# Score-value products of a paired head moved to the front of the next head, pairs of groups with fewer joins in other banks, and inverse roots' steps on GpSimd

## Chip, cores and metric

The kernel runs on one core of one Trainium2 chip. The metric is the device time of one execution in microseconds. Five engines of the core matter: TensorE (PE, with its weight loads as PEld), VectorE (DVE), ScalarE (ACT), GpSimd (POOL) and SyncE (SP, which here only issues loads).

## What is computed

A decoder trunk of two layers on 256 tokens of width 2048: first gated linear attention (GLA, 4 heads), then retention (8 heads), each after an RMS norm and with a SiLU gate; a residual add ends each layer and an RMS norm ends the trunk. Cut to what the change touches, a retention layer is

```
proj = rms_norm(h) @ w_in                    # q, k, v, gate
q, k = rotary(q), rotary(k)
o = (causal decay mask * (q @ k.T)) @ v      # per head, chunkwise in the reference
o = (o - mean(o)) * rsqrt(var(o) + EPS)      # per head, the "inverse root"
o = o * gn_g + gn_b
h = h + (o * silu(gate)) @ w_out
```

A GLA head has an inverse root too, rsqrt(mean(o*o) + EPS).

## The kernel before

**Weights and splits.** All weight matrices lie in DRAM as groups of 512 output columns. A group has 16 tiles of 128x512 (4 MB). SP loads it in chunks of 4 tiles (`raw`, four buffers). A chunk is cut into two units of 2 tiles. Each unit is split into a high and a low part in a rounded 32-bit type: ACT copies `hi` (L216), DVE subtracts to give `lo` (L217), both into pools of three buffers. The product of x and w is then three matmuls, xh·hi, xh·lo and xl·hi, in this order within a bank (L277 to L279 in pairs, L256 to L258 in plain groups). Splits are issued two units ahead of their use (`LOOK`).

**Pairs.** Two groups p and q that multiply the same input are done with seven block products in place of eight (`pair_x`), with token halves as rows and the first half of the contraction as the part that is recombined. `PAIR` is the order by hand: blocks `S1` to `S7` are one product of 12 matmuls each (two units), blocks `V0` to `V3` and `G0` to `G3` are plain products of one unit for both token halves, 12 matmuls each. Four results are wanted: 11 and 21 of group p, 12 and 22 of group q. Some block products are needed in several results, so they are taken out of PSUM and added elsewhere. These additions are called joins here. They are driven by events ("p1" after S1, "q" after S5, "p2" after S6, "p3" after S7, and "11", "21", "12", "22" when a bank is complete). PSUM has eight banks: pool `acc` with four, `lev` with two, `mis` with two. Where S5 or S6 need it, the weights of q are added onto the raw chunk of p in SBUF by an accumulating DMA that POOL issues (L225), after the split that last read the chunk. `token_combos` makes the recombined inputs.

**Where pairs are used.** In both output projections (`out_half`: "ga" and "gb" after GLA, "ra" and "rb" after retention, seven pairs in all, results added into the residual `R["t"]`) and in six retention heads (`paired`: h = 0, 1, 2, 4, 5, 6), where p is the value group and q the gate group. Heads 3 and 7 do the two groups in the plain way.

**A retention head.** `group_w` makes q and k of the head in eight units of 16 matmuls (units j = 0 to 7). `evac_w` takes them out of PSUM. `ret_scores` (rotary products L1040 to L1045, score matmuls, mask) runs as a generator on the `side` queue, a step at each `advance()`. Then the pair gives value and gate. The score-value products (`o_mms`, nine matmuls), the norm, the inverse root (`rsqrt`, L439 to L444, then L1114), the scaling (L1116) and `og_part` (gate product L1124, eight transposes L651, split L657 and L658 into `ogt`) of a paired head are held in `waiting` and run inside the `group_w` of the next head, at j = 3. GLA heads do their inverse root in `og_part` at L835.

**Order.** The order on each engine is fixed when the program is built: a scheduler walks the operations with priorities, so a later operation can be put ahead of an earlier one on the same engine. On the chip each engine takes its instructions strictly in that order. POOL's queue holds accumulating DMAs of weights, loads of small tables (L1047, L1093, L1094, L937), copies of the residual and 14 additions for each GLA head (L782).

## Time and profile before

| | before |
|---|---|
| median of 3 runs | 1401.64 us (1401.49 to 1404.17) |
| profiled execution, its own time | 1399.42 us |
| its span, first to last instruction | 1397.6 us |
| PE busy | 1372.5 us (98%) |
| DVE busy | 1070.9 us (77%) |
| ACT busy | 797.1 us (57%) |
| POOL busy | 144.7 us (10%) |
| mean granted TensorE clock | 0.998 |

The profiled execution took 1.8 us more than its span. A matmul's end in the profile is modelled: a 512-column matmul shows about 0.39 us although the next one can start 0.23 us after it, so the idle time that the profile gives for PE is a little shorter than what a stop costs.

### The profile page before, as it was taken

The page shows a single profiled execution, that of the slowest core. Times are in us where ns is not written, and L with a number is a line of the kernel's source. Part 1 is how long each engine was busy: PE and PEld are TensorE (multiplying, and loading weights), DVE is VectorE, ACT ScalarE, POOL GpSimd, SP SyncE. Part 2 cuts the span into 40 slices and gives each one's busy share as a digit, 9 for nine tenths or more (in the row PEclk, how much of TensorE's full clock was granted, in tenths as well). Part 3 has the DMA queues.
Part 4 walks back from the last instruction along what each step waited for, and adds up shares of the span by engine and source line. Part 5 has one row for each costly group of instructions (what it writes and reads, how often), then busy time and mean ns, then how long its engine had stood idle before and what let it go on. Part 6 is the DMA issues. An engine that isn't in the chain of part 4 may idle for free.

```text
span 1397.6 us, 17891 instructions
## 1 busy us (share of the span) xinstructions
PE 1372.5 (98%) x6644; PEld 1147.9 (82%) x6644; DVE 1070.9 (77%) x1619; ACT 797.1 (57%) x1012; POOL 144.7 (10%) x209
## 2 busy tenths in 40 slices
PE   8999999999999999999999999999999999999997
PEld 7888888788888888887887878888787878788887
DVE  6595798787845784888878787898777888888783
ACT  6665655755555646665665656456556565645563
POOL 1000030110010020111011111001201010100200
PEclk9999999999999999999999999999999999999999
DMA  9554555898545555799796969569989797974981
GB/s 370 192 185 147 193 180 181 203 296 266 174 175 181 185 195 183 188 297 277 231 276 201 273 202 304 208 198 268 278 291 237 238 234 240 233 306 165 234 297 61
DMA packets 54631, 316.04 MB, mean 226 GB/s; under 512 B 6400, under 2 KB 6912, under 8 KB 25232
## 3 DMA queue, kind: packets, MB, share of 16 engines
q1 hardware_dynamic: 34944, 243.42, 48.4%
q0 software_dynamic: 18592, 70.13, 24.7%
q10 hardware_dynamic: 1008, 1.35, 0.3%
q8 instruction: 52, 0.85, 0.2%
q14 instruction: 35, 0.29, 0.1%
HBM read 308.58 MB, written 6.29 MB: 225 GB/s over the span
## 4 chain that ended last, share of the span: by engine, by line
PE 92%; DVE 3%; DMA 2%; ACT 2%; issue 1%; ACTq 0%; POOLq 0%; DVEq 0%
PE rqk_ps L420 8%; PE rp__ps L278 4%; PE rp__ps L279 4%; PE gv_ps L256 4%; PE rp__ps L277 4%; PE gv_ps L257 4%; PE gv_ps L258 4%; PE gg_ps L256 4%; PE gg_ps L258 4%; PE gg_ps L257 4%; PE rqk_ps L421 4%; PE gqk_ps L420 4%; PE gqk_ps L421 2%; DMA raw<-in_w_all 2%; DVE lo L217 2%; ACT hi L216 1%
## 5 line engine op out<-in xcount | busy, mean ns | idle before, releaser
L216 ACT ACTIVATE hi<-raw 128x1024 fp32r<-128x1024 f32 (+1 forms) x551 | 580.0, 1058 | 503.4 <-PE rp__ps L279 80.8
L217 DVE TENSOR_TENSOR lo<-raw,hi 128x1024 fp32r<-128x1024 f32 (+1 forms) x551 | 666.0, 1222 | 256.2 <-ACT hi L216 251.6
L420 PE MATMUL rqk_ps<-xhl,hi 128*128 128x512 f32 x480 | 161.5, 394 | 0.0
L225 POOL DMA_DIRECT2D raw<-in_w_all x104 | 88.4, 850 | 470.0 <-DVE lo L217 430.8
L421 PE MATMUL rqk_ps<-xhl,lo 128*128 128x256 f32 x480 | 120.9, 280 | 0.0
L420 PEld LDWEIGHTS rqk_ps<-xhl,hi 128*128 128x128 f32 x480 | 88.0, 188 | 16.8
L257 PE MATMUL gv_ps<-lo,xhl 128*128 128x512 f32 x256 | 100.4, 392 | 0.0
L257 PE MATMUL gg_ps<-lo,xhl 128*128 128x512 f32 x256 | 100.4, 392 | 0.0
L258 PE MATMUL gv_ps<-hi,xhl 128*128 128x512 f32 x256 | 100.3, 392 | 0.0
L258 PE MATMUL gg_ps<-hi,xhl 128*128 128x512 f32 x256 | 100.0, 391 | 0.0
L278 PE MATMUL rp__ps<-lo,xhl 128*128 128x512 f32 x240 | 94.1, 392 | 2.6 <-DVE lo L217 2.6
L279 PE MATMUL rp__ps<-hi,xhl 128*128 128x512 f32 x240 | 93.5, 389 | 0.0
L256 PE MATMUL gv_ps<-hi,xhl 128*128 128x512 f32 x256 | 93.0, 391 | 0.0
L421 PEld LDWEIGHTS rqk_ps<-xhl,lo 128*128 128x128 f32 x480 | 87.8, 188 | 5.0
L256 PE MATMUL gg_ps<-hi,xhl 128*128 128x512 f32 x256 | 91.7, 391 | 0.0
L277 PE MATMUL rp__ps<-hi,xhl 128*128 128x512 f32 x240 | 85.2, 390 | 2.8 <-ACT hi L216 2.8
L420 PE MATMUL gqk_ps<-xhl,hi 128*128 128x512 f32 x216 | 72.4, 396 | 0.0
L782 POOL TENSOR_TENSOR s<-s,m 128x64 f32<-128x64 f32 x56 | 32.3, 610 | 241.5 <-DVE m L773 230.8
L278 PEld LDWEIGHTS rp__ps<-lo,xhl 128*128 128x128 f32 x240 | 45.1, 188 | 13.6 <-DVE lo L217 4.6
L257 PEld LDWEIGHTS gv_ps<-lo,xhl 128*128 128x128 f32 x256 | 48.1, 188 | 9.7
L257 PEld LDWEIGHTS gg_ps<-lo,xhl 128*128 128x128 f32 x256 | 48.1, 188 | 9.6
L258 PEld LDWEIGHTS gg_ps<-hi,xhl 128*128 128x128 f32 x256 | 48.1, 188 | 9.6
(461 smaller groups left out, 2694.3 us busy)
## 6 DMA issues: line engine op xcount, KB each, us to landing
raw<-in_w_all SPq DMA_DIRECT2D x225, 1024.0 KB, 4.9
raw<-in_w_all POOLq DMA_DIRECT2D x104, 512.0 KB, 7.2
held<-resid POOLq DMA_DIRECT2D x4, 1024.0 KB, 10.5
resid<-held POOLq DMA_DIRECT2D x2, 2048.0 KB, 12.2
resid<-in_x_n SPq DMA_DIRECT2D x2, 1024.0 KB, 11.2
gg<-in_gn_g POOLq DMA_DIRECT2D x8, 256.0 KB, 3.8
gb<-in_gn_b POOLq DMA_DIRECT2D x8, 256.0 KB, 4.5
raw<-in_w_all SPq DMA_DIRECT2D x3, 512.0 KB, 6.1
```

Source lines behind the costliest of these rows:

```text
L216: a = nc.scalar.activation(hi[:, sl], src[:, sl], AF.Copy)
L217: b = nc.vector.tensor_tensor(lo[:, sl], src[:, sl], hi[:, sl].bitcast(F32), ALU.subtract)
L225: nc.gpsimd.dma_start(src, chunk_src(g, k)[:, rows], accum_op=ALU.add)
L256: mm(ps, xh, hi[:, q, :], start=kt == 0, stop=False)
L257: mm(ps, xh, lo[:, q, :], start=False, stop=False)
L258: mm(ps, xl, hi[:, q, :], start=False, stop=kt == NKT - 1)
L277: mm(ps, xh, hi[:, q, :], start=start, stop=False, skip_group_check=True)
L278: mm(ps, xh, lo[:, q, :], start=False, stop=False, skip_group_check=True)
L279: mm(ps, xl, hi[:, q, :], start=False, stop=stop, skip_group_check=True)
L420: mm(ps[c], wh, rhs[:, kt, :, :], start=kt == 0, stop=False)
L421: mm(ps[c][:, 0, :], wl, rhs[:, kt, 0, :], start=False, stop=False)
L782: nc.gpsimd.tensor_tensor(dst, dst, side_of(m[:, li, :]), ALU.add)
```

## The change

The score-value products and all that follows them for a paired head are called at j = 0 of the next head's `group_w` in place of j = 3. The order of a pair puts V0 ahead of S2, and V0 does its second token half first. The first block product is copied by ACT from its bank into the bank of result 11, where V and S2 then accumulate, and result 22 accumulates in the bank that holds the product of S5. So the separate join of "p1" and one of the two joins of "q" are gone in `out_half`. In paired heads two DVE additions (in "p3" and "11") are gone, and the split of v's first half reads PSUM. The three steps of the iteration in `rsqrt` for GLA and retention heads run on GpSimd, four instructions a step in place of three on DVE, and so does the product L1114.

```diff
@@ -117,7 +117,7 @@
         for j in range(raws_per_group):
             plan_units(plan_chunk(g, j))
 
-    PAIR = ("S1", "S2", "V0", "V1", "S5", "S3", "V2", "G0", "S6", "G1", "S7", "V3", "S4", "G2", "G3")
+    PAIR = ("S1", "V0", "S2", "V1", "S5", "S3", "V2", "G0", "S6", "G1", "S7", "V3", "S4", "G2", "G3")
 
     def plan_pair(gp, gq):
         at = {}
@@ -342,16 +342,18 @@
         def mixed(n):
             return lambda k: tuple(x[:, k] for x in combos[cname][n])
 
-        def both(ps, j, start, stop):
+        def both(ps, j, start, stop, second_first=False):
             hi, lo = next_weights()
-            for q in range(SUB):
-                for t in range(2):
-                    kt = 2 * CHUNK + j * SUB + q
-                    x = tuple(lhs[:, kt, i, t * P : (t + 1) * P] for i in range(2))
-                    product(ps[t], x, hi, lo, q, start[t] and q == 0, stop[t] and q == SUB - 1)
+            order = [(q, t) for q in range(SUB) for t in range(2)]
+            if second_first:
+                order = [(q, t) for t in (1, 0) for q in range(SUB)]
+            for q, t in order:
+                kt = 2 * CHUNK + j * SUB + q
+                x = tuple(lhs[:, kt, i, t * P : (t + 1) * P] for i in range(2))
+                product(ps[t], x, hi, lo, q, start[t] and q == 0, stop[t] and q == SUB - 1)
             advance()
 
-        c21 = b = c12 = c22 = None
+        c21 = b = c12 = None
         for block in PAIR:
             kind, n = block[0], int(block[1])
             if kind == "V":
@@ -359,21 +361,20 @@
                     c21 = acc_p.tile([P, GW], F32, tag="acc", name=f"{name}_ps21")
                 if n == 2 and late is not None:
                     late()
-                both((c11, c21), n, (False, n == 0), (n == 3, False))
+                both((c11, c21), n, (False, n == 0), (n == 3, False), n == 0)
                 if n == 3:
                     on("11", c11)
             elif kind == "G":
-                if c22 is None:
-                    c22 = lev_p.tile([P, GW], F32, tag="lev", name=f"{name}_ps22")
-                both((c12, c22), n, (False, n == 0), (n == 3, n == 3))
+                both((c12, b), n, (False, False), (n == 3, n == 3))
                 if n == 3:
                     on("12", c12)
-                    on("22", c22)
+                    on("22", b)
             elif n == 1:
                 seven(a, plain(0, 0), True, True)
-                on("p1", a)
+                with tc.high_priority():
+                    nc.scalar.activation(c11, a, AF.Copy)
             elif n == 2:
-                seven(c11, plain(1, 0), True, False)
+                seven(c11, plain(1, 0), False, False)
             elif n == 5:
                 while cname not in combos:
                     advance()
@@ -433,15 +434,21 @@
                 nc.scalar.activation(tmp[:, c, :], ps[c][:, 1, :], AF.Copy)
                 nc.vector.tensor_tensor(dst[:, c, :], ps[c][:, 0, :], tmp[:, c, :], ALU.add)
 
-    def rsqrt(y, m, n, name):
+    def rsqrt(y, m, n, name, eng=None):
         s = st_p.tile([P, 4, n], F32, tag="nw", name=f"{name}_nw")
         a, b = s[:, 0, :], s[:, 1, :]
         nc.vector.tensor_scalar(a.bitcast(I32), m.bitcast(I32), 1, None, ALU.logical_shift_right)
         nc.vector.tensor_scalar(b.bitcast(I32), a.bitcast(I32), -1, 0x5F3759DF, ALU.mult, ALU.add)
         for it in range(3):
-            nc.vector.scalar_tensor_tensor(a, b, -0.5, m, ALU.mult, ALU.mult)
-            nc.vector.tensor_tensor(a, a, b, ALU.mult)
-            nc.vector.scalar_tensor_tensor(y if it == 2 else b, a, 1.5, b, ALU.add, ALU.mult)
+            if eng is None:
+                nc.vector.scalar_tensor_tensor(a, b, -0.5, m, ALU.mult, ALU.mult)
+                nc.vector.tensor_tensor(a, a, b, ALU.mult)
+                nc.vector.scalar_tensor_tensor(y if it == 2 else b, a, 1.5, b, ALU.add, ALU.mult)
+            else:
+                eng.tensor_tensor(a, b, m, ALU.mult)
+                eng.tensor_tensor(a, a, b, ALU.mult)
+                eng.tensor_scalar(a, a, -0.5, 1.5, ALU.mult, ALU.add)
+                eng.tensor_tensor(y if it == 2 else b, a, b, ALU.mult)
 
     def split_scaled(dst, src, scale):
         nc.scalar.activation(dst[:, 0], src, AF.Copy, scale=scale)
@@ -832,7 +839,7 @@
                 hr = st_p.tile([P, 2], F32, tag="hr", name=f"hr{h}")
                 nc.vector.tensor_tensor(m, sso[:, :, 0], sso[:, :, 1], ALU.add)
                 nc.vector.tensor_scalar(m, m, 1.0 / 1024.0, EPS, ALU.mult, ALU.add)
-                rsqrt(hr, m, 2, f"hr{h}")
+                rsqrt(hr, m, 2, f"hr{h}", nc.gpsimd)
                 hw["hr"] = hr
                 yield
             o, sg, hr = os_[gj], sgs[gj], hw["hr"]
@@ -908,11 +915,8 @@
                     with tc.high_priority():
                         nc.vector.tensor_tensor(dst, dst, ps, op)
 
-                if event == "p1":
-                    join(0, 0, ALU.add)
-                elif event == "q":
+                if event == "q":
                     join(0, 1, ALU.subtract)
-                    join(1, 1, ALU.add)
                 elif event == "p2":
                     join(0, 1, ALU.subtract)
                 elif event == "p3":
@@ -1073,7 +1077,7 @@
         paired = h % 4 < 3
 
         def late_o(j):
-            if j == 3 and waiting:
+            if j == 0 and waiting:
                 waiting.pop()()
 
         ps = group_w(xhl, f"rqk{h}", hook=late_o)
@@ -1110,8 +1114,8 @@
             a = st_p.tile([P, 2], F32, tag="hr", name=f"ra_{h}")
             nc.vector.tensor_tensor(m, mv[:, :, 1], r2, ALU.mult)
             nc.vector.tensor_scalar(m, m, EPS, None, ALU.add)
-            rsqrt(a, m, 2, f"rh{h}")
-            nc.vector.tensor_tensor(a, a, r, ALU.mult)
+            rsqrt(a, m, 2, f"rh{h}", nc.gpsimd)
+            nc.gpsimd.tensor_tensor(a, a, r, ALU.mult)
             for t in range(2):
                 nc.vector.scalar_tensor_tensor(
                     o[:, t, :], o[:, t, :], a[:, t : t + 1], gb, ALU.mult, ALU.add
@@ -1148,30 +1152,25 @@
         tt = nc.vector.tensor_tensor
 
         def on(event, ps):
-            if event == "p1":
+            if event == "q":
+                with tc.high_priority():
+                    nc.scalar.activation(sg[:, 0, :], ps, AF.Copy)
+            elif event == "p2":
+                with tc.high_priority():
+                    tt(sg[:, 0, :], ps, sg[:, 0, :], ALU.add)
+            elif event == "p3":
                 with tc.high_priority():
                     nc.scalar.activation(o[:, 0, :], ps, AF.Copy)
-            elif event == "q":
-                nc.scalar.activation(sg[:, 1, :], ps, AF.Copy)
-            elif event == "p2":
+            elif event == "11":
+                split_scaled(v[:, 0], ps, r2[:, 0:1])
+            elif event == "21":
                 with tc.high_priority():
-                    tt(sg[:, 0, :], ps, sg[:, 1, :], ALU.add)
-            elif event == "p3":
-                with tc.high_priority():
-                    nc.scalar.activation(o[:, 1, :], ps, AF.Copy)
-                    tt(sg[:, 1, :], ps, sg[:, 1, :], ALU.add)
-            elif event[1] == "1":
-                t = int(event[0]) - 1
-                with tc.high_priority():
-                    tt(o[:, t, :], ps, o[:, t, :], ALU.subtract if t else ALU.add)
-                nc.scalar.activation(v[:, t, 0, :], o[:, t, :], AF.Copy, scale=r2[:, t : t + 1])
-                nc.vector.scalar_tensor_tensor(
-                    v[:, t, 1, :], o[:, t, :], r2[:, t : t + 1], v[:, t, 0, :].bitcast(F32), ALU.mult, ALU.subtract
-                )
+                    tt(o[:, 1, :], ps, o[:, 0, :], ALU.subtract)
+                split_scaled(v[:, 1], o[:, 1, :], r2[:, 1:2])
             else:
                 t = int(event[0]) - 1
                 with tc.high_priority():
-                    tt(sg[:, t, :], ps, sg[:, t, :], ALU.add if t else ALU.subtract)
+                    tt(sg[:, t, :], ps, (o if t else sg)[:, 0, :], ALU.add if t else ALU.subtract)
                 keep(nc.scalar.activation(sg[:, t, :], sg[:, t, :], AF.Silu, scale=r[:, t : t + 1]))
 
         pair_x(xhl, f"rp{h}_", "x1" if h < 4 else "x2", on)
```

## Rows read from the trace of the kernel before

**Rows 1.** The page: busy us by engine (share of the span), instructions.
```profile
PE 1372.5 (98%) x6644; PEld 1147.9 (82%) x6644; DVE 1070.9 (77%) x1619; ACT 797.1 (57%) x1012; POOL 144.7 (10%) x209
```

**Rows 2.** Waits of PE over the span: who waited for whom, us, times, longest.
```profile
PE rp__psb L277 <- ACT hi L216: 3.9, 4, 1.0
PE rp__ps L277 <- ACT hi L216: 2.8, 2, 1.4
PE rp__ps L278 <- DVE lo L217: 2.6, 4, 0.7
...
PE ra_ps L277 <- ACT hi L216: 1.6, 1, 1.6
PE gb_psa L277 <- ACT hi L216: 0.7, 1, 0.7
PE ga_ps L277 <- ACT hi L216: 0.6, 1, 0.6
PE gb_ps L278 <- DVE lo L217: 0.6, 2, 0.4
PE ga_ps L278 <- DVE lo L217: 0.5, 1, 0.5
```

**Rows 3.** Timeline of PE at the pair of head 0: start, us, instruction.
```profile
687.99 0.39 PE L279 MATMUL rp__psa<-hi,xhl 128*128 128x512 f32 x1
688.22 0.39 PE L277 MATMUL rp__ps<-hi,xhl 128*128 128x512 f32 x1
690.01 0.50 PE L277 MATMUL rp__ps<-hi,xhl 128*128 128x512 f32 x1 [1.41 <-ACT hi L216]
```

**Rows 4.** Timeline of DVE at the same place.
```profile
686.57 1.23 DVE L1040 TENSOR_TENSOR ra<-rqk,trig 128x1024 f32<-128x1024 f32 x1
...
688.32 0.69 DVE L1043 TENSOR_TENSOR rb<-rqk,trig 128x512 f32<-128x512 f32 x1
688.92 2.35 DVE L217 TENSOR_TENSOR lo<-raw,hi 128x1024 fp32r<-128x1024 f32 x2
```

**Rows 5.** Timeline of ACT at the same place.
```profile
685.98 2.15 ACT L216 ACTIVATE hi<-raw 128x1024 fp32r<-128x1024 f32 x2
688.42 0.60 ACT L1153 ACTIVATE ro<-rp__psa 128x512 f32<-128x512 f32 x1 [0.29 <-PE rp__psa L279]
```

**Rows 6.** Timeline of PE at the pair of head 1.
```profile
754.05 0.38 PE L651 MATMUL rot_tp<-ident,ro 128*128 128x128 f32 x2
...
758.51 0.50 PE L278 MATMUL rp__ps<-lo,xhl 128*128 128x512 f32 x1 [0.65 <-DVE lo L217]
...
762.72 0.50 PE L277 MATMUL rp__psb<-hi,x_d 128*128 128x512 f32 x1 [0.97 <-ACT hi L216]
```

**Rows 7.** Timeline of DVE in the `group_w` ahead of it.
```profile
743.10 0.17 DVE L439 TENSOR_SCALAR rh_nw<-rm 128x2 int32<-128x2 int32 x1
...
747.97 0.16 DVE L1114 TENSOR_TENSOR ra<-ra,r 128x2 f32<-128x2 f32 x1
...
751.24 0.68 DVE L1124 TENSOR_TENSOR ro<-ro,rsg 128x512 f32<-128x512 f32 x1
```

**Rows 8.** Groups of DVE by line and form: count, busy us, mean ns.
```profile
L217 DVE TENSOR_TENSOR lo<-raw,hi 128x1024 fp32r<-128x1024 f32 x549 | 664.6, 1224 | 256.2 <-ACT hi L216 251.6
...
L909 DVE TENSOR_TENSOR resid<-resid,gb_psa 128x512 f32<-128x512 f32 x8 | 5.3, 682 | 0.3 <-PE gb_psa L279 0.3
...
L442 DVE SCALAR_TENSOR_TENSOR rh_nw<-rh_nw,rm 128x2 f32<-128x2 f32 x24 | 3.9, 161 | 0.8
```

**Rows 9.** The additions on POOL: durations in ns, least, median, most.
```profile
L782 POOL TENSOR_TENSOR s<-s,m x56: 312/330/4589, 101.5 to 513.7; 128x64 f32<-128x64 f32 x56
```

**Rows 10.** Timeline of POOL at the additions of GLA head 1.
```profile
190.04 10.20 POOL L782 TENSOR_TENSOR s<-s,m 128x64 f32<-128x64 f32 x14 [33.82 <-DVE m L773]
```

**Rows 11.** Timeline of DVE at the same place.
```profile
190.89 2.39 DVE L287 TENSOR_TENSOR ga_f<-ogt 128x1024 f32<-128x1024 f32 x2
193.16 1.26 DVE L217 TENSOR_TENSOR lo<-raw,hi 128x1024 fp32r<-128x1024 f32 x1
```

## Prediction

> **What bounds the kernel now.** I read the page first: PE is busy 98% of the span [rows 1] at a granted clock of 0.998, which is its upper level of 2.4 GHz. The change neither adds nor removes a matmul, since every block product keeps its 12, so the work of PE stays as it is and only the stops of PE can be won or lost. The second view is therefore what PE waits for. Between the start-up and the tail it lists ten waits inside the pairs of the retention heads, 3.9 + 2.8 + 2.6 = 9.3 us, and six in the output projections, 1.6 + 0.7 + 0.6 + 0.6 + 0.5 = 4.0 us [rows 2]. A stop costs more than its idle time: with matmuls starting 0.23 us apart, the one that should have followed 688.22 started at 690.01, 1.56 us late, while the row counts 1.41 us idle [rows 3]. So each stop gets 0.16 us on top: 10.9 us in the heads, 5.0 us in the projections, 15.9 us in all. That is 1.1% of the time and the most that the change could give.
>
> The third view is the timelines of these stops. In head 0 the stop comes right after S1. PE does the first high product of S2, then needs the low part of that unit. DVE makes it from 688.92 on, because the three rotary products that start at 686.57 and end at 689.0 stand ahead of it in DVE's order [rows 4], although its high part was there after the first of the two splits that ACT began at 685.98, about 687.0 [rows 5]. Head 4 repeats this, which gives the two waits of 1.4. Heads 1, 2, 5 and 6 show two stops each: the same place with 0.65 us idle, and one of 0.97 us before the first product of S5 [rows 6], four times each in the waits [rows 2]. There the eight transposes of the head before lie inside S1 [rows 6], so PE reaches the end of S1 later and waits less for the low part. The second stop is a product that stands early in PE's order, whose high part ACT had not made yet.
>
> **The change, part by part.**
>
> The call at j = 0 in place of j = 3. It moves three units of `group_w` earlier: a unit is 8 x (0.23 + 0.12) = 2.8 us of PE (the 256-column matmul taken at half), so up to 8.3 us. In the trace the gate product ended at 751.92 [rows 7], and the first two transposes ran at 754.05 [rows 6], already in S1. After the change they can run before S1, and their splits (four on ACT, four on DVE) with them. Then all six heads enter their pair as head 0 does. The second stop, which head 0 lacks, goes: 4 x (0.97 + 0.16) = 4.5 us won. The first one grows to head 0's, 1.56 in place of 0.65 + 0.16 = 0.81, since the transposes no longer fill it: 4 x 0.75 = 3.0 us lost. The transposes themselves cost the same elsewhere. Nothing else on SP's or POOL's queues is passed: the held work issues no DMA. Two loads of norm tables (L1093, L1094) wait for buffers that it frees, and these come free earlier.
>
> V0 ahead of S2. V0's unit is now the one whose low part is late. In each bank the high product stands first, so PE can do one in bank 21 and one in bank 11 before it needs the low part, against one in S2: 6 x 0.23 = 1.4 us won. The rest of the stop stays, because the rotary products are still ahead of the low part on DVE. Bounds: nothing, if DVE's order is as it was, and the whole 6 x 1.56 = 9.4 us, if the scheduler puts that low part first. I take the 1.4 us, nearer to the first, since head 0 shows this order without any held work in its way. S1 and V0 ask for three splits in the time in which S1 and S2 asked for four (a low part takes 1.22 us [rows 8], a block of 12 matmuls 2.7 us), so no new shortage arises there. Sum for the heads: -4.5 + 3.0 - 1.4 = -2.9 us.
>
> The copy into bank 11. ACT reads and writes PSUM; the nearest row is its copy of the same bank to SBUF, 0.60 us, begun at 688.42 [rows 5], 0.43 us after the last matmul of S1 started [rows 3]. It would end at 689.02. The six products of V0 in bank 21 cover it until 688.22 + 6 x 0.23 = 689.6. That is 0.56 us of room in each of 13 pairs, so I take nothing in most. If a split (1.05 us, half of the double row [rows 5]) is ahead of it, it is up to 0.5 us late: upper bound 13 x 0.5 = 6.5 us. A few such cases: +0.3 us. In the heads ACT had this copy already; in the projections it is new and takes the place of a DVE join.
>
> Fewer joins. Two of six go in each of seven projection pairs, 2 x 0.68 us of DVE [rows 8]. DVE is not the bound on the whole, so this is worth something only where PE stood for DVE or for a split behind it: the "gb" stops, 0.7 + 0.6 and three times 0.16, 1.8 us. I take half, -0.9 us; bounds 0 and -1.8. The stops in "ga" and "ra" wait for splits of chunks that land late, and here the new order is no help: the chunk of S2 is now split one unit later and its buffer is given back later. I leave them as they are; the bound is one S unit, 1.4 us, in each of three first pairs. In paired heads two DVE additions go, at the end of V3 and S7, where PE shows no stop: nothing.
>
> Inverse roots on GpSimd. Nine small DVE operations at 0.16 us [rows 8] (and L1114) become twelve or thirteen on POOL in each of twelve heads. No row shows an operation of this size on POOL. The nearest is the addition over 64 elements: median 0.33 us [rows 9], but 14 of them took 10.20 us in one head [rows 10], 0.73 us each. There the first one started at 190.04 and lasted 4.59 us [rows 9], until the end of four DVE operations back to back, all with two inputs in SBUF [rows 11]: POOL stands while DVE runs those. The Trainium skill says this in "SBUF — State Buffer", section "Who interferes with whom": a DVE instruction with two SBUF inputs contends with a GpSimd instruction that reads SBUF, and whoever issues second waits for the whole instruction. The trace agrees with it: 4.59 us in place of 0.33 us [rows 9 to 11]. With the roots held up by that rule as far as these rows go, 15 us in the sum below would stand in place of 0.4 us; with none of it, 0. The chain on POOL is then 13 x 0.33 = 4.3 us at best and 13 x 0.73 = 9.5 us at worst, against 4.9 us on DVE (743.10 to 747.97 with the splits between [rows 7]). Later by -0.6 to +4.6 us. Behind it wait the two scalings, the gate product and the transposes, and on DVE the splits that stand behind the scaling. The room to the transposes was 754.05 - 751.92 = 2.1 us, and the six paired heads start up to 8.3 us earlier now. So in these it costs nothing. In the six other heads it costs up to 4.6 - 2.1 = 2.5 us each, 15 us; I take the middle of the chain, which fits in the room, and 0.4 us for the cases over it.
>
> **Sum.** -2.9 + 0.3 - 0.9 + 0.4 = -3.1 us. The profiled execution of 1399.42 becomes 1396.3. It lies 2.2 us under the median of the runs, so the median goes from 1401.64 to 1398.5 us.
>
> **Rivals.**
>
> All entry stops go. If the scheduler also places the low part of V0 before the rotary products, 10.9 us of the heads and 0.9 us of the projections go: 1390 us. For it: the high part was ready before two of the three rotary products started. Against it: the same order in all six heads, with and without held work.
>
> The stops only change place. The held products and their statistics now fall on the end of the pair and the first units of `group_w`, and another unit is late there by what was won: 1401.6 us, give or take 2. For it: DVE has little slack anywhere in the retention part. Against it: `group_w` has no PE stop in the list now.
>
> The roots come too late. If POOL is held up as in the trace [rows 10], by about one more low part of 1.22 us than the room allows, DVE stands at the scaling, and splits and transposes behind it stop PE. At 1.2 us in each of twelve heads this is +14 us on the sum, 1413 us. It decides against the change from about 0.5 us a head (6 us against the 3.1 won). For it: the chain can reach 9.5 us. Against it: when DVE stands, it no longer holds POOL up, and a unit is split well ahead of its use.
>
> The copy is late. With a split ahead of it in all pairs, +6.5 us on the sum: 1405 us.
>
> **How the numbers follow.** A measurement of this kernel can tell about 0.2%, 2.8 us, from no change, so 1398.8 to 1404.4 us counts as the same. The sum's own case gets 0.45 (0.31 of it faster, 0.14 the same, own range 1395 to 1401). All stops gone 0.15, faster. Stops that change place 0.18, the same. Late roots 0.14 and late copies 0.08, slower. That makes 0.46, 0.32 and 0.22. The range of 1390 to 1407 takes in all stops gone and late copies, and leaves out the worse half of late roots.
>
> **What would show it.** Right: no transposes of `rot_tp` inside S1, no wait of `rp__psb` for `hi`, a remaining stop of some 1.3 us right after S1 in all six heads with the rotary products before the low part on DVE, the wait for the copy absent from PE's list, PE's work unchanged. Wrong: waits of DVE L1116 or L840 for POOL of several us with PE stops behind them, PE waiting for ACT's copy, or a `lo` ahead of L1040 at the entry (then more is won than I say).

## The result

The change made the kernel slower. The median went from 1401.57 us (four runs) to 1413.43 us (four runs, 1410.38 to 1413.88), a ratio of 1.0078 with a 95% interval of 1.0057 to 1.0099. The forecast was 1398.5 us with a range of 1390 to 1407, so the sign was wrong and the time lies outside the range. The profiled execution took 1413.74 us with a span of 1412.0 us at a clock of 0.997.

The page of the changed kernel (busy us, share of the span, instructions) against [rows 1]:

```profile
PE 1380.2 (98%) x6644; PEld 1149.6 (81%) x6644; DVE 1037.8 (74%) x1477; ACT 800.6 (57%) x1019; POOL 190.6 (13%) x361
```

PE has the same 6644 matmuls as before. DVE lost 142 instructions and 33 us, POOL gained 152 instructions and 46 us, as the change says. DVE is less busy and the kernel is slower, so the time is in stops. The waits of PE (who waits for whom: us in total, times, longest us), against [rows 2]:

```profile
PE rp__ps L278 <- DVE lo L217: 5.8, 9, 1.0
PE ra_ps L277 <- ACT hi L216: 4.0, 2, 3.1
PE rp__ps L277 <- ACT rp__ps L375: 2.9, 6, 0.5
PE ga_ps L277 <- ACT hi L216: 2.1, 2, 1.4
...
PE gb_ps L278 <- DVE lo L217: 1.5, 4, 0.8
PE ra_ps L278 <- DVE lo L217: 0.8, 1, 0.8
PE ga_ps L278 <- DVE lo L217: 0.8, 1, 0.8
PE rb_ps L278 <- DVE lo L217: 0.8, 1, 0.8
PE gb_ps L277 <- ACT gb_ps L375: 0.5, 1, 0.5
PE rb_ps L277 <- ACT hi L216: 0.4, 1, 0.4
PE rot_tp L658 <- DVE ro L1128: 0.2, 1, 0.2
```

The four waits of `rp__psb` for `hi` are gone, as forecast. But the list, without the start-up, now holds 29 waits of 19.8 us, where before it held 16 of 13.3 us. With the 0.16 us that each stop costs beyond its idle time, as the prediction takes it, that is 24.4 us in place of 15.9, 8.5 us more. The new ones are waits for the copy into bank 11, more waits for low parts in the heads, and long ones in the projections, 3.1 us in "ra" the longest. That list says that splits come late, not why. For that one looks at what ScalarE itself waited for before it split a chunk. In the kernel before this row reads:

```profile
ACT hi L216 <- DMA raw<-in_w_all: 8.9, 7, 2.6
```

and in the changed kernel:

```profile
ACT hi L216 <- DMA raw<-in_w_all: 54.0, 34, 3.9
```

So chunks of weights reach their split late 34 times, not 7 times. Most of this wait is idle time that PE never sees, because splits run ahead of their use; where the lead is used up it becomes a stop. So this total says where to look and does not measure the loss: further down, a version without a measurable loss waits 48.1 us.

### The profile page after: what moved, and what is told of

Same layout as the page of the kernel before. It is cut to its first block, busy times and chain, and to the rows that moved or that the text cites. A ratio compares the mean times of both kernels' runs of the same rounds, so it can differ in the third digit from the quotient of the medians.

```text
span 1412.0 us, 17904 instructions
## 1 busy us (share of the span) xinstructions
PE 1380.2 (98%) x6644; PEld 1149.6 (81%) x6644; DVE 1037.8 (74%) x1477; ACT 800.6 (57%) x1019; POOL 190.6 (13%) x361
## 3 DMA queue, kind: packets, MB, share of 16 engines
q10 hardware_dynamic: 1008, 1.35, 0.3%
## 4 chain that ended last, share of the span: by engine, by line
PE 74%; DMA 11%; DVE 7%; issue 4%; ACT 3%; POOL 1%; ACTq 0%; POOLq 0%; DVEq 0%
DMA raw<-in_w_all 11%; PE rqk_ps L421 8%; PE gv_ps L256 4%; PE gv_ps L257 4%; PE gv_ps L258 4%; DVE lo L217 4%; PE gg_ps L256 4%; PE rqk_ps L422 4%; PE gg_ps L258 4%; PE gg_ps L257 4%; PE gqk_ps L421 3%; ACT hi L216 2%; PE rp__ps L278 2%; PE rp__ps L279 2%; PE rp__ps L277 2%
## 5 line engine op out<-in xcount | busy, mean ns | idle before, releaser
L278 PE MATMUL rp__ps<-lo,xhl 128*128 128x512 f32 x192 | 75.8, 395 | 5.8 <-DVE lo L217 5.8
L279 PE MATMUL rp__ps<-hi,xhl 128*128 128x512 f32 x192 | 74.8, 390 | 0.0
L277 PE MATMUL rp__ps<-hi,xhl 128*128 128x512 f32 x192 | 71.7, 394 | 2.9 <-ACT rp__ps L375 2.9
L257 PEld LDWEIGHTS gv_ps<-lo,xhl 128*128 128x128 f32 x256 | 48.1, 188 | 9.7
L257 PEld LDWEIGHTS gg_ps<-lo,xhl 128*128 128x128 f32 x256 | 48.1, 188 | 9.6
L256 PEld LDWEIGHTS gv_ps<-hi,xhl 128*128 128x128 f32 x256 | 47.9, 188 | 9.9
L258 PEld LDWEIGHTS gg_ps<-hi,xhl 128*128 128x128 f32 x256 | 48.1, 188 | 9.6
```

The lines of the kernel that those rows point to most:

```text
L256: mm(ps, xh, hi[:, q, :], start=kt == 0, stop=False)
L257: mm(ps, xh, lo[:, q, :], start=False, stop=False)
L258: mm(ps, xl, hi[:, q, :], start=False, stop=kt == NKT - 1)
L277: mm(ps, xh, hi[:, q, :], start=start, stop=False, skip_group_check=True)
L278: mm(ps, xh, lo[:, q, :], start=False, stop=False, skip_group_check=True)
L279: mm(ps, xl, hi[:, q, :], start=False, stop=stop, skip_group_check=True)
```

## The experiments

All kernels were compared with the kernel before on the same chip. "Order" below means the kernel before with `PAIR` changed to S1, V0, S2, ..., V0 doing its second half first and opening bank 11 itself, and nothing else changed: no copy, joins as before, DVE roots, held work at j = 3.

**Which part of the change costs.** Four kernels: each of three parts alone on the kernel before, and the changed kernel with the old order and no copy.

```diff
--- late alone
-            if j == 3 and waiting:
+            if j == 0 and waiting:
--- order alone
-    PAIR = ("S1", "S2", "V0", "V1", "S5", ...)
+    PAIR = ("S1", "V0", "S2", "V1", "S5", ...)
-                seven(c11, plain(1, 0), True, False)
+                seven(c11, plain(1, 0), False, False)
--- roots alone
-            rsqrt(a, m, 2, f"rh{h}")
-            nc.vector.tensor_tensor(a, a, r, ALU.mult)
+            rsqrt(a, m, 2, f"rh{h}", nc.gpsimd)
+            nc.gpsimd.tensor_tensor(a, a, r, ALU.mult)
--- changed kernel, old order, no copy (S1 is joined as before)
-    PAIR = ("S1", "V0", "S2", "V1", "S5", ...)
+    PAIR = ("S1", "S2", "V0", "V1", "S5", ...)
-                    nc.scalar.activation(c11, a, AF.Copy)
+                on("p1", a)
```

> The kernel before with one part of the change: the score-value products of a paired head are called at j = 0 of the next head in place of j = 3. Theory order (V0 ahead of S2 gives buffers of raw chunks back later, so loads land late): this part does no harm; the second stop of heads 1, 2, 5 and 6 goes, 1396 to 1401 us. Theory roots (the chain on GpSimd is late and holds DVE and PE up): the same, 1396 to 1401 us. If the moved call alone costs time (statistics fall on a busier stretch): above 1404 us.

> The kernel before with the order S1, V0, S2 of a pair alone (V0's second token half first; V0 starts bank 11, so no copy; all joins as before; inverse roots on DVE). Theory order: most of the loss is here, 1406 to 1414 us, with ACT waiting for raw chunks some 40 us in all in place of 9 us. Theory roots: within 2 us of before. Theory copy (PE waits for ACT's copy into bank 11): within 3 us of before.

> The kernel before with the inverse roots' steps on GpSimd alone. Theory roots: 1409 to 1415 us, with DVE waiting for POOL some 16 us and PE stops behind. Theory order and theory copy: 1400 to 1404 us; DVE waits for POOL, but PE has no new stop.

> The changed kernel with the old order S1, S2, V0 and without the copy into bank 11 (its first block product is joined as before); the moved call, result 22 in the bank of S5 and the roots on GpSimd stay. Theory order or theory copy: the loss is gone, 1395 to 1403 us. Theory roots: it stays, 1408 us or more.

| kernel | median us | ratio to before (95%) |
|---|---|---|
| late call alone | 1402.21 | 1.0014 (1.0001 to 1.0028) |
| order alone | 1410.47 | 1.0061 (1.0040 to 1.0083) |
| roots alone | 1404.64 | 1.0024 (1.0011 to 1.0037) |
| changed, old order, no copy | 1403.88 | 1.0028 (1.0015 to 1.0040) |

At 1401.6 us a thousandth is 1.4 us: order 8.5 us, roots 3.4 us, late call 2.0 us. Their sum, 13.9 us, is at the upper end of the interval of the whole change (8.0 to 13.9 us). Taken the other way, the changed kernel with the old order and no copy loses 3.9 us in place of 10.9. The order is the main cost. The late call and the last kernel came out about 1 us above their expected ranges, and the roots between the two that were expected.

*The late call.* The waits of PE with the late call alone:

```profile
PE rp__ps L277 <- ACT hi L216: 8.4, 6, 1.4
```

All six paired heads now enter their pair as heads 0 and 4 did [rows 3], with one stop of 1.4 us, and the second stop is gone. That is what I had forecast, -4.5 and +3.0 us. The whole list of this run has 13 stops of 13.1 us, 15.2 us with the 0.16 us each, against 15.9 before. Yet the balance measured is between 0.1 and 3.9 us of loss. Where that loss lies the list does not show; it stays open.

*The roots.* POOL in the `group_w` ahead of the pair of head 1, with the roots alone (start us, us, instruction, in brackets the idle time before):

```profile
745.64 0.22 POOL L447 TENSOR_TENSOR rh_nw<-rh_nw,rm 128x2 f32<-128x2 f32 x1
745.93 1.16 POOL L448 TENSOR_TENSOR rh_nw<-rh_nw 128x2 f32<-128x2 f32 x1
747.19 0.19 POOL L449 TENSOR_SCALAR rh_nw<-rh_nw 128x2 f32<-128x2 f32 x1
...
748.84 1.05 POOL L447 TENSOR_TENSOR rh_nw<-rh_nw,rm 128x2 f32<-128x2 f32 x1
...
750.81 0.20 POOL L1120 TENSOR_TENSOR ra<-ra,r 128x2 f32<-128x2 f32 x1
```

and DVE beside it:

```profile
745.82 1.23 DVE L217 TENSOR_TENSOR lo<-raw,hi 128x1024 fp32r<-128x1024 f32 x1 [0.39 <-ACT hi L216]
748.61 1.23 DVE L217 TENSOR_TENSOR lo<-raw,hi 128x1024 fp32r<-128x1024 f32 x1 [1.56 <-ACT hi L216]
751.04 1.41 DVE L1122 SCALAR_TENSOR_TENSOR ro<-ro,ra,gb 128x512 f32<-128x512 f32 x2 [1.20 <-POOL ra L1120]
```

An operation takes 0.20 us where POOL is free, and the next starts 0.28 us after its start. Two of the thirteen lasted 1.16 and 1.05 us, each until the end of a low part on DVE that had started just before it (747.05 and 749.84). The Trainium skill, "SBUF — State Buffer", section "Who interferes with whom", says that a DVE instruction with two SBUF inputs contends with a GpSimd instruction that reads SBUF. These rows agree with it. The chain took 5.4 us, and DVE stood 1.20 us at the scaling behind it. Over the span DVE waits 19.3 us for the ends of these chains, 10.4 us in retention heads and 8.9 us in the four GLA heads:

```profile
DVE ro L1122 <- POOL ra L1120: 10.4, 8, 2.3
DVE go L846 <- POOL hr L450: 8.9, 4, 3.4
```

Most of that PE never sees. It shows at the entry of the pairs, in place of 2.6 us [rows 2]:

```profile
PE rp__ps L278 <- DVE lo L217: 4.3, 4, 1.1
```

**What the order does to the transfers.** The view is the timeline of SP's queue and of POOL at the pair of head 1, and then the DMA issues of a window with the median us from issue to landing. In the kernel before S1 starts at 753.81:

```profile
759.62 4.47 SPq L183 DMA_DIRECT2D raw<-in_w_all  x2
```

```profile
765.82 0.84 POOL L225 DMA_DIRECT2D raw<-in_w_all  x1 [11.26 <-DVE lo L217]
```

```profile
raw<-in_w_all SPq DMA_DIRECT2D x2, 1024.0 KB, 4.7
```

```profile
raw<-in_w_all POOLq DMA_DIRECT2D x4, 512.0 KB, 5.7
```

With the order alone S1 starts at 756.41:

```profile
765.21 2.12 SPq L183 DMA_DIRECT2D raw<-in_w_all  x2
```

```profile
769.35 0.84 POOL L225 DMA_DIRECT2D raw<-in_w_all  x1 [12.19 <-DVE lo L217]
```

```profile
raw<-in_w_all SPq DMA_DIRECT2D x2, 1024.0 KB, 6.0
```

```profile
raw<-in_w_all POOLq DMA_DIRECT2D x4, 512.0 KB, 9.1
```

Read from the start of S1, the pair's first plain load goes out at +5.8 us before and at +8.8 us with the order. (The rows merge neighbouring issues: the second load goes out at 763.76 and at 767.01.) S2's chunk is split one unit later, and V0's chunk is held until V1, behind S2, so the first buffer comes free 3 us later. The second load follows at +10.6 us (before: +9.9). The two accumulating transfers behind S1's splits go out ahead of S1 in both kernels (751.62 and 753.71 before). The next four, two behind S5's splits and two behind S3's, begin at +12.0 before and at +12.9 now. Before, the two loads landed 4.8 and 4.6 us after their issue, at 764.4 and 768.4, so only the second still ran when these four began. With the order they took 4.8 and 7.2 us and landed at 770.0 and 774.2, beside the first three of the four. And S5's two are now 1.1 us apart in place of 2.4. The four take 9.1 us, not 5.7 (median). In the changed kernel they take 9.2 us. S6 and S7 read what they bring. Over the span, ScalarE's wait for chunks in the order alone is

```profile
ACT hi L216 <- DMA raw<-in_w_all: 63.8, 40, 3.9
```

That is a coincidence in time so far. The next three sets of runs test it.

**Half of the accumulating transfers.** The kernel before and the order, with half of each accumulating transfer left out (so their results are not those of the layer):

```diff
-            nc.gpsimd.dma_start(src, chunk_src(g, k)[:, rows], accum_op=ALU.add)
+            nc.gpsimd.dma_start(src[:, :, 0 : GW // 2], chunk_src(g, k)[:, rows, 0 : GW // 2], accum_op=ALU.add)
```

> The kernel before, with each accumulating DMA of weights on half of its columns (256 KB in place of 512 KB; the other half of q's weights is left out of the sums). It is the control for the next run. All theories: 1394 to 1402 us, since ACT waits little for raw chunks in the kernel before (9 us).

> The order S1, V0, S2 alone, with the accumulating DMAs on half of their columns as in the run beside it. Theory collision (the order gives a buffer back some 3 us later, so two loads run beside the accumulating DMAs, these land late, and the splits of S3, S6 and S7 wait for them): with half the bytes they land in time, ACT's wait for raw chunks falls from 64 us to under 20 us, and the order costs under 3 us against the run beside it. Theory entry (the order itself costs at the entry of a pair on PE and DVE): the order still costs 6 us or more against it.

The control took 1398.04 us, a ratio of 0.9972 (0.9962 to 0.9982). With the order it took 1390.9 us, 0.9916 (0.9900 to 0.9933). The loss of 8.5 us has become a gain of 7.1 us. The order's own work on PE and on the splits is thus a gain, and the loss comes with the accumulating transfers at full size. ScalarE's wait for chunks is 2.0 us in the control and 5.3 us with the order:

```profile
ACT hi L216 <- DMA raw<-in_w_all: 5.3, 5, 1.8
```

**Half of the two plain loads.** The runs above show that these transfers matter, not what makes them late. Here the accumulating transfers are whole, and only the chunks of V2 and G0, the two loads in question, fetch half of their columns, which the splits then use twice.

```diff
+            cols = slice(0, GW // 2) if c in half_loads else slice(0, GW)
-            nc.sync.dma_start(t[:, sl, :], src[:, sl, :])
+            nc.sync.dma_start(t[:, sl, cols], src[:, sl, cols])
...
+            if c in half_loads:
+                x = x[:, :, 0 : GW // 2].unsqueeze(2).to_broadcast([P, step, 2, GW // 2])
```

> Control for the next run: the kernel before, in which the two plain loads of 1 MB that each pair issues just ahead of its first accumulating transfers (the chunks of V2 and of G0) fetch half of the columns, and the splits use that half twice, so half of those weights is left out. Splits, products and accumulating transfers are as before. In the kernel before the first accumulating transfers landed in 5.6 to 5.8 us there, beside little else. All theories: 1396 to 1401 us, at most 0.3% faster.

> The order S1, V0, S2 with the same two loads at half of their columns (half of those weights is left out). Theory: the order makes these two loads late and puts them beside the pair's first accumulating transfers, which then take 8 to 10 us. With half of the bytes these transfers land in 6 to 7 us again, ScalarE's waits for chunks fall from 64 us to under 25, and the loss of the order (8.5 us against the kernel before) goes: within 2 us of the control or faster, down to -7. Rival: the accumulating transfers are late for a reason of their own (their buffers, their queue, their issue), and the plain loads only happen to be near: landing times of 8 to 10 us and a loss of 6 to 10 us against the control stay.

The control took 1401.04 us, 1.0007 (0.9992 to 1.0021); its profiled execution had a stop of 4.4 us in "ra", where the kernel before has one of 1.6 us, so the medians are compared and not the spans. The order took 1395.71 us, 0.9959 (0.9944 to 0.9974), 5.3 us faster than its control. At the pair of head 1 the first four accumulating transfers of the order land in

```profile
raw<-in_w_all POOLq DMA_DIRECT2D x4, 512.0 KB, 7.5
```

and ScalarE's wait for chunks falls from 63.8 us to

```profile
ACT hi L223 <- DMA raw<-in_w_all: 25.4, 19, 3.5
```

where under 25 us had been expected. The loss is gone, so the rival in its strong form, in which a loss of 6 to 10 us stays, falls. But the landing time did not come down to the 6 to 7 us expected. The control has 5.7 us there, as the kernel before, so of the 3.4 us by which the order delays these four, 1.6 us go with half of the loads. The rest is not all due to the half that is left: the last two of the four go out when both loads have landed, and take 7.7 and 9.3 us, against 5.7 and 8.8 us in the control. A delay of their own is thus part of it. Both halvings also take bytes off the queues as a whole; in the next runs all bytes are moved.

**Loads back in their place.** If V1 follows V0 at once, both units of that chunk are split early and its buffer comes free before S2.

```diff
-    PAIR = ("S1", "V0", "S2", "V1", "S5", ...)
+    PAIR = ("S1", "V0", "V1", "S2", "S5", ...)
```

> The kernel before with the order S1, V0, V1, S2: V0 is still ahead of S2, but V1, which reads the other half of V0's chunk, comes right behind it, so that its buffer comes free before S2's chunk is begun, as in the kernel before. Theory buffers: the loss of the order goes, 1397 to 1404 us, ACT waits for raw chunks under 25 us. If V0 ahead of S2 costs by what PE needs at the entry of a pair: 1406 us or more.

> The changed kernel, whole, with the order S1, V0, V1, S2. Theory buffers: the roots and the moved call keep their 2 to 4 us, the order's loss goes: 1401 to 1405 us. If the copy into bank 11 is a cause of its own, it stays above 1407 us.

On the kernel before, without the rest of the change, this took 1399.6 us, 0.9989 (0.9970 to 1.0008): no loss. The whole change with it took 1405.79 us, 1.0037 (1.0021 to 1.0053), in place of 1.0078. The first load at the pair of head 1 goes out at +5.8 us after S1 again, as before, and ScalarE's wait is 33.5 us, between the two. So the same blocks in an order that gives a buffer back early cost nothing, with all bytes moved. The landing time is not the simple cause of this, though. At the pair of head 1 the same four transfers are as slow in this order as in the one that loses:

```profile
raw<-in_w_all POOLq DMA_DIRECT2D x4, 512.0 KB, 9.4
```

S5's two go out 1.1 us apart here too. Over all 13 pairs the median of these four (52 transfers) is 7.3 us in the kernel before, 9.2 us in the order alone, 8.0 us here, 8.0 us in the order with half loads and 7.0 us in its control. So both ways of taking the loads out of the way bring back half of the delay or somewhat more, and with that the loss is gone. That the rest comes from transfers that follow each other more closely is argued from these times; no run changed the spacing alone. ScalarE's wait had been expected under 25 us, and the whole change at 1405 us or less.

**More and smaller buffers.** Two attempts to get the loads early in another way failed.

```diff
--- five buffers (with room made for the fifth)
-    raw_p = pool("raw", 4)
+    raw_p = pool("raw", 5)
--- eight buffers of one unit, loads of 512 KB
-        t = raw_p.tile([P, CHUNK, GW], F32, tag="raw", name=f"raw{c}")
+        t = [raw_p.tile([P, SUB, GW], F32, tag="raw", name=f"raw{c}_{h}") for h in range(per_raw)]
```

> The kernel with the order S1, V0, S2 alone (as in the second run), and five raw buffers in place of four; to make room, the scratch of the DMAs that POOL issues is 2 KB in place of 8 KB. Theory buffers (two half-used chunks hold buffers, so the next loads start late): ACT's wait for raw chunks falls from 64 us to under 20 us, the long stops in the output projections go, and the time falls from 1410 to 1399 to 1403 us. If it stays above 1408 us and the waits stay, the loss is in the order of the products on PE, not in the buffers.

> Control for the run with five buffers: the order S1, V0, S2 alone with four raw buffers and the scratch of 2 KB. All theories: as the order alone, 1407 to 1413 us; if it is much higher, the small scratch costs time itself and the run with five buffers has to be read against this one.

> The order S1, V0, S2 alone with five raw buffers again, with the constants at the places of the kernel before (in the first run with five buffers they had moved and every 512-column matmul started 0.233 us after the last in place of 0.227 us); only the scratch of POOL's DMAs is 2 KB in place of 8 KB. Theory collision: a fifth buffer brings chunks one load earlier but leaves the loads at the times at which splits give buffers back, so they still run beside the accumulating DMAs: ACT still waits over 40 us, 1403 to 1410 us, with only the long stops in the output projections (waits for SP's loads) gone. Theory buffers in its first form (chunks themselves come late): 1398 to 1402 us.

> The kernel before with raw buffers of one unit (2 tiles, 512 KB) in place of one chunk: eight buffers in the same space, two loads a chunk. Each half is given back when its own unit is split. It is the control for the next two runs. Theory collision: little changes, 1396 to 1404 us. If twice as many loads of half the size cost by themselves: above 1405 us.

> The order S1, V0, S2 alone with raw buffers of one unit. Now V0's half is given back before S2, so no load has to wait for V1. Theory collision with late buffers as its root: the accumulating DMAs land in 7.5 us or less at the median, ACT waits for raw chunks under 30 us, and the order's own gain at the entry of a pair shows: 1390 to 1398 us. If the accumulations are late for another reason (they are issued later and closer to each other in this order): they still take over 8 us, and the time stays above 1404 us.

> The order S1, V0, S2 with raw buffers of one unit and fewer joins (result 22 in the bank of S5), the first block product joined, the held products at j = 3, roots on DVE. Theory collision: at or up to 2 us under the run beside it, 1388 to 1398 us. If fewer joins cost (as the run with S1, V0, V1, S2 and fewer joins, 1.5 us over that order alone, may say): 1 to 4 us over it.

The first pair of runs made its room by moving constants in SBUF, which cost far more than what was to be measured (1420.36 us with five buffers, 1421.07 us with four; more of this in the last section). With the constants in place, the order with five buffers took 1409.97 us, 1.0056 (1.0035 to 1.0076), as slow as with four. The loads go out at the same moments after S1 as with four, because they still wait for the same splits; each only fetches the chunk after. Their collision stays, and ScalarE's wait is 79.8 us.

With unit buffers the kernel before itself got slower, 1415.57 us, 1.0092 (1.0060 to 1.0124); ScalarE waited 56.7 us for chunks, and its accumulating transfers landed in a median of 8.0 us over the span, against 7.2 us in the kernel before. The order on top took 1432.25 us, 1.0222 (1.0199 to 1.0246), and the same order with result 22 in the bank of S5, and so with fewer joins, 1428.09 us, 1.0185 (1.0150 to 1.0219). V0 and V1 together were not tried with unit buffers. A buffer that comes free after each unit did not cure the loss but raised it, to 17 us over its control, which is a miss for the account that the late buffer alone is at fault: 1390 to 1398 us had been expected. What the many smaller loads do to the accumulating transfers was not taken apart; it stays open.

**The copy, and a best version.**

```diff
--- changed kernel, no copy: V0 opens bank 11, S1 is joined as before
-                with tc.high_priority():
-                    nc.scalar.activation(c11, a, AF.Copy)
+                on("p1", a)
--- kernel before, V0 and V1 together, result 22 in the bank of S5
-    PAIR = ("S1", "S2", "V0", "V1", "S5", ...)
+    PAIR = ("S1", "V0", "V1", "S2", "S5", ...)
-                both((c12, c22), n, (False, n == 0), (n == 3, n == 3))
+                both((c12, b), n, (False, False), (n == 3, n == 3))
```

> The changed kernel without the copy into bank 11: V0 starts the bank and the first block product is joined as before. Theory collision alone: the copy is no cause, 1409 to 1415 us. Theory copy as a second cause (0.67 us at the entry of each pair in the trace of the changed kernel): 1404 to 1409 us.

> A version from the parts that did no harm: the order S1, V0, V1, S2, result 22 in the bank of S5 with its joins gone, the first block product joined as before (no copy into bank 11), the held products at j = 3, inverse roots on DVE. Theory collision: 1394 to 1400 us, faster than before by up to 0.4%. If the fewer joins are worth nothing: as the order S1, V0, V1, S2 alone, within 2 us of before.

Without the copy the changed kernel took 1412.78 us, 1.0076 (1.0048 to 1.0103), against 1.0078 with it: no effect of the copy and of the joins that it saves is measured, though one of 2 or 3 us either way would be lost in these intervals. V0 and V1 together, result 22 in the bank of S5, DVE roots and the call at j = 3 took 1401.1 us, 0.9992 (0.9980 to 1.0004), although ScalarE waits 48.1 us for chunks in it, 31 times. No version tried is measurably faster than the kernel before while it moves all of the weights.

## Why the prediction was wrong

**The step that failed.** It is in the part on V0 ahead of S2: "S1 and V0 ask for three splits in the time in which S1 and S2 asked for four [...] so no new shortage arises there", and, further on, of the chunk of S2 whose buffer is given back later: "I leave them as they are; the bound is one S unit, 1.4 us, in each of three first pairs." I counted splits and took their data as given. I saw the late buffer and priced it as a delay of one unit, once, in the projections. But a load that goes out 3 us late does not only arrive 3 us late. It runs beside what is issued next, here the accumulating transfers, of which there are eight in a pair and which four of the seven S blocks read. Where no shortage was forecast, ScalarE waited for chunks 40 times, 63.8 us with the order alone, in place of 7 times, 8.9 us. The four transfers behind S5 and S3 went from a median of 7.3 to 9.2 us over all pairs. That the loss needs the loads and these transfers at full size, and goes with the loads back in their place, is shown; the loads account for half of the delay in landing or somewhat more, and the cause of the rest stays open. The order was taken as -1.4 us and measured +8.5 us (5.6 to 11.6). The rows that would have warned of it stood in the trace before: the issue times on SP's and POOL's queues. The forecast does not set them against the blocks of a pair.

**The late call**: the mechanism was right. The second stop went, and the first grew to 1.4 us in all six heads. Its size was off in two ways. At the pair of head 1 the transposes moved from 0.2 us behind the start of S1 (754.05, S1 at 753.81) to 1.8 us ahead of it (753.36, S1 at 755.17), 2 us and not up to 8.3 us, since in PE's order they still stand in the last unit ahead of S1; and the balance of -1.5 us measured +2.0 us (0.1 to 3.9), by something that the list of stops does not hold.

**V0's extra high product**: it is seen with the order alone. PE does two high products (from 760.06) and then waits less for the low part, against 0.65 us [rows 6]:

```profile
760.06 0.63 PE L277 MATMUL rp__ps<-hi,xhl 128*128 128x512 f32 x2
761.10 0.50 PE L278 MATMUL rp__ps<-lo,xhl 128*128 128x512 f32 x1 [0.42 <-DVE lo L217]
```

So it is in heads 1, 2, 5 and 6, 0.23 us each as forecast; in heads 0 and 4 the stop went from 1.41 to 1.36 us, some 1.0 us in all in place of 1.4. The waits of `rp__psb` are gone with the order alone too, although the transposes still stand inside S1 there. The forecast gave those 4.5 us to the late call; the order wins them by itself, so the two gains do not add. In the changed kernel this entry became two stops. PE at the pair of head 1:

```profile
756.53 0.82 PE L658 MATMUL rot_tp<-ident,ro 128*128 128x128 f32 x6
...
761.68 0.39 PE L277 MATMUL rp__ps<-hi,xhl 128*128 128x512 f32 x1
762.58 0.50 PE L277 MATMUL rp__ps<-hi,xhl 128*128 128x512 f32 x1 [0.51 <-ACT rp__ps L375]
764.06 0.50 PE L278 MATMUL rp__ps<-lo,xhl 128*128 128x512 f32 x1 [0.98 <-DVE lo L217]
```

and DVE at the same place, against [rows 4]:

```profile
760.45 1.22 DVE L1044 TENSOR_TENSOR ra<-rqk,trig 128x1024 f32<-128x1024 f32 x1
761.58 0.69 DVE L1045 TENSOR_TENSOR rb<-rqk,trig 128x512 f32<-128x512 f32 x1
762.18 0.69 DVE L1047 TENSOR_TENSOR rb<-rqk,trig 128x512 f32<-128x512 f32 x1
762.78 2.36 DVE L217 TENSOR_TENSOR lo<-raw,hi 128x1024 fp32r<-128x1024 f32 x2
```

No transpose stands inside S1 and the three rotary products are still ahead of the low part, both as forecast.

**The copy**: I took +0.3 us because six products of V0 in bank 21 would cover it. They do not run: PE does one high product at 761.68 and the next one in its order, at 762.58, is already in the copy's bank, so PE stands for the copy, 0.5 us in six heads, and then, one product later, 0.98 us for the low part. As PE would stand for the low part anyway, little of it is lost, which agrees with the run without the copy.

**The roots**: 0.4 us forecast, 3.4 us (1.5 to 5.2) measured. The chain of 5.4 us lies inside my bounds of 4.3 to 9.5 us. The mistake was to count the room before the transposes as free: DVE stood 1.20 us at the scaling, and the splits behind it entered the pair late. The sign of being wrong that I named, waits of DVE for POOL of several us, came: 7.0 us in the retention heads and 8.9 us in the GLA heads of the changed kernel. The rival of late roots gave 1413 us, and so came out at the measured time, but by a chain that the run of the roots alone shows to be a quarter of that.

**Fewer joins**: no gain is seen (-0.9 us forecast). In "gb" the waits of the changed kernel are 2.0 us against 1.3 us before. Two pairs of runs above differ in the joins and the saved additions alone: 0.9992 against 0.9989 with V0 and V1 together, and 1.0185 against 1.0222 with unit buffers. The first shows nothing, and the intervals of the second overlap.

**Rest.** In the profiled executions the span grew by 14.4 us. The stops of the list account for 8.5 us, the lower clock in "ra" (below) for about 1.6 us, and 0.9 us lies in the start-up, which differs as much between kernels that are the same there. The other 3.4 us are not attributed.

## What to carry to other kernels

When an order written by hand is changed, redo the count for the buffers too: for each chunk find the instruction that frees its buffer, the load that waits for it, and what is on the queues when that load now runs. A load moved by 3 us can cost nothing by itself and still slow the transfers that it runs beside, and their consumers pay. And look at more than one pair: a single pair can show the same delay in a version that loses and in one that does not. A chain of small operations that goes to an idle engine is not free either if a busy engine reads its end: what the chain is late counts for all that stands behind the reader.

## What the runs showed of the hardware

**A stop that is paid twice.** After the long stop in "ra" PE ran slower for a while. The changed kernel, windows of the profile (us, PE busy and matmuls, PEld, DVE, ACT, POOL, granted clock, DMA share, GB/s):

```profile
1008.00:1012.00 4.00, 0.90 (x4) 0.67 (x4) 0.83 (x1) 1.92 (x2) 0.00 (x0) 1.00 1.06 219
1012.00:1015.00 3.00, 3.00 (x9) 2.32 (x8) 1.53 (x2) 0.08 (x1) 0.84 (x1) 0.52 0.99 197
1015.00:1020.00 5.00, 5.00 (x23) 4.08 (x22) 1.98 (x2) 2.61 (x3) 0.83 (x1) 0.95 0.72 120
```

and PE's timeline there:

```profile
1007.69 0.40 PE L279 MATMUL ra_ps<-hi,c_d 128*128 128x512 f32 x1
1011.19 0.50 PE L277 MATMUL ra_ps<-hi,ogt 128*128 128x512 f32 x1 [3.10 <-ACT hi L216]
...
1012.34 0.63 PE L278 MATMUL ra_ps<-lo,ogt 128*128 128x512 f32 x1
1012.77 0.63 PE L279 MATMUL ra_ps<-hi,ogt 128*128 128x512 f32 x1
...
1015.65 0.40 PE L278 MATMUL ra_ps<-lo,ogt 128*128 128x512 f32 x1
```

PE stood 3.10 us, resumed at the upper level of 2.4 GHz, and 1 us later fell to the lower one of 1.2 GHz (0.52 in that window): matmuls start 0.43 us apart in place of 0.23 us. The nine matmuls from 1012.00 to 1015.65 take 3.65 us where they would take 2.07 us, 1.6 us on top of the 3.1 us. The order alone fell to the lower level at its own stop of 3.1 us there (0.50 from 1008 to 1012 us), and the control with half of the plain loads at its stop of 4.4 us. The kernel before, whose stop in "ra" is 1.6 us [rows 2], kept its clock.

**Moved constants slowed the matmuls.** In the first two runs on buffers one table of constants was made smaller, so that what lies behind it in SBUF moved, and the 512-column matmuls got slower. The group of one of them in the kernel before:

```profile
L257 PE MATMUL gv_ps<-lo,xhl 128*128 128x512 f32 x256 | 100.4, 392 | 0.0
```

and in the order with four buffers and moved constants:

```profile
L257 PE MATMUL gv_ps<-lo,xhl 128*128 128x512 f32 x256 | 101.9, 398 | 0.0
```

In a stretch without stops (80 to 240 us) PE has 779 matmuls in the one and 765 in the other. The order alone with constants in their old places took 1.0061 of the kernel before and this control 1.0138, some 10 us more for a move that no view of waits shows. The two kernels with five buffers differ in that table alone: 765 matmuls where it is smaller, 779 where it has its old size. What about the places does it was not tried.
